# Gathering the tokens of a mixture of experts in four chunks of plain fp32, with nothing of the next stage emitted amid the experts

## The chip, the cores and the metric

One core of one Trainium2 chip runs the whole kernel. Its engines are TensorE (PE, with its weight loads PEld), VectorE (DVE), ScalarE (ACT), GpSimd (POOL) and SyncE (SP), which issues most DMAs. The metric is the device time of one execution in microseconds (us), the median of several runs.

## What is computed

256 tokens of width 1024 pass through ten stages. Stages 0 to 5 are two transformer blocks of a first kind (SwiGLU, token mixer, SwiGLU, twice). Stages 6 to 9 are a second kind: attention, mixture of experts (MoE), attention, MoE. Each stage is modulated by a vector that is a product of a conditioning vector with a 1024x6144 matrix (`ada_w`). All weights are fp32 in HBM. The MoE, of which the change speaks:

```
h = rms_norm_2(x, norm_ffn_g[i]) * (1.0 + sc2) + sh2
x = x + g2 * grouped_moe(h, router_w, router_bias, moe_w_gate[i], moe_w_up[i], moe_w_down[i])

def grouped_moe(h, ...):
    scores = sigmoid(t @ router_w)          # 16 experts; one group, top 2 inside it
    ...
    for e in range(N_EXPERTS):
        he = silu(t @ w_gate[e]) * (t @ w_up[e])
        out = out + gates[:, e:e + 1] * (he @ w_down[e])
```

Each expert has 1024x512, 1024x512 and 512x1024 weights, so a MoE stage reads 192 pieces of 512 KB.

## The kernel before

**Order.** Nothing is left to a scheduler: each engine runs its instructions in the order in which the Python code emits them, and an engine waits at an instruction until its operands and its target buffer are ready.

**Weights as a stream.** Weights come as "units" of 128x1024 fp32 (512 KB) in the order of use, through one pool of equal buffers (`s4`, `S4_BUFS` of them, 4 KB in each partition). SP issues the loads (line 76, tile `raw`). Three kinds of unit follow each other:

- Normal units are split in two: ACT makes `hi` (line 117) and DVE `lo` (line 122); PE then takes three products of one pass each (lines 325 to 327).
- Units of `ada_w` are worked off by DVE alone (line 414, or 412 for the first of a vector: multiply and add into `aacc`). When a vector is complete, PE sums it over the partitions (line 421).
- Units of the experts are plain: PE multiplies by them as they are.

`stream.ahead(n)` splits up to n units that have been loaded and loads further ones as long as the pool has more free buffers than `self.reserve`; of units that are not plain, only a few wait loaded and unsplit. `pump()` calls it after each step with a credit that grows by `self.rate`. A second pool (`t2`, 2 KB in each partition, `T2_BUFS`) holds small tiles.

**The MoE stages (7 and 9).** `route` normalises x to `xn`, computes the scores and lays the tokens into 16 x 64 slots: a slot table that says which of 256 tokens sits in which slot. Two experts make a pair (128 slots), two pairs a chunk of 256 slots. A chunk is gathered by multiplying the tokens by a one-hot matrix `OH`; the product goes through ACT or DVE (modulation) into `hg`. Before the change xn is split into two parts of one-pass precision, `xs` (`high` on ACT, line 1833; `low` on DVE, line 1837), and each of the eight k steps of a chunk takes four one-pass matmuls of 256 columns (line 1660). Chunk 0 is gathered ahead of the pairs, chunks 1 to 3 amid them. The DMA of xn to HBM (`xd`, line 1943, on ACT's queue, four of them) and of the row of the gate `g2` (`row`, line 449) stand around there as well.

`pairs` then emits eight pairs. For pair j: `G(j)`, the gate product of 32 matmul instructions (line 1575); `X(j-1)`, transposes of the pair before; G again for the up product; `Dn(j-1)`, the down product (line 1594, 32 instructions); and what adds pair j-1 into x: `Y` (lines 1602 to 1608) and `S` (PE line 1615, then DVE `x <- x + psacc`, line 1617). Gathering steps and S steps wait in a queue, of which `tick` takes one after every quarter (8 instructions) of a G or a Dn. After pair 7 come X(7), Dn(7) and a tail: the S of pair 6, and Y and S of pair 7, after which x is complete. Then the next stage normalises x, transposes it (line 376) and starts with its products.

Of the kernel before, what the change touches and what calls it, by code (L numbers as in the profile page):

```python
# [11 lines left out]
F32 = mybir.dt.float32  # L12
# [9 lines left out]
P = 128  # L22
D = 1024
# [9 lines left out]
S4_BUFS = 39  # L33
T2_BUFS = 14
# [148 lines left out]
class Net:  # L183
# [261 lines left out]
    def row(self, st):  # L445

        self.need(st, "row")
        r = self.s4([P, D], F32, "row")
        self.nc.sync.dma_start(r, self.rowd.pop((st, "row")).rearrange("a b -> (a b)").partition_broadcast(P))
        return r  # L450
# [757 lines left out]
    def proj_halves(self, st, hT):  # L1208
# [32 lines left out]
        self.rate, self.reserve = 0, 17  # L1241
# [318 lines left out]
    def pairs(self, hg, gsl, row, OHT, done):  # L1560
# [90 lines left out]

    def gather(self, c, OH, xs, hg, G, S):

        nc = self.nc
        s = slice(c * 256, (c + 1) * 256)
        for k in range(KC):
            ps = self.ps()
            for t in range(NT):
                for i in range(2):
                    nc.tensor.matmul(ps[:, :256], xs[i][t][:, k * P:(k + 1) * P], OH[t][:, s], start=t == 0 and i == 0, stop=t == 1 and i == 1)  # L1660
# [7 lines left out]
            yield  # L1668

    def slots(self, c, OH, gates, gsl, OHT):  # L1670

        nc = self.nc
        pg = self.ps()
        for i in range(2):
            j = 2 * c + i
            for t in range(NT):
                nc.tensor.matmul(pg[:, 2 * i:2 * i + 2], OH[t].bitcast(F32)[:, j * P:(j + 1) * P], gates[:, t, 2 * j:2 * j + 2], start=t == 0, stop=t == 1)
# [111 lines left out]
    def moe(self, st, pre, rest):  # L1789
# [10 lines left out]
        xn, xT, r, ss, junk, xs = {}, {}, {}, {}, {}, {}  # L1800
# [68 lines left out]
        high(0, 0)  # L1869
# [4 lines left out]
        low(0, 0)  # L1874
        high(0, 1)
# [38 lines left out]
        low(1, 0)  # L1914
# [41 lines left out]
        OHT = [self.s4([P, 4, 256], F32R, "OHT") for _ in range(2)]  # L1956
        self.reserve = 1
        gsl = self.sm(8, name="gsl", bufs=1)
        box = {}
        for c in range(4):  # L1960
            if c:
                self.side.append(lambda c=c: [hot(t, c) for t in range(NT)])
# [167 lines left out]
```

## Time and profile before

| what | us |
|---|---|
| median of 3 runs | 2264.72 (2261.26 to 2264.96) |
| profiled execution | 2252.76 |
| its span, first to last instruction | 2251.1 |
| PE busy | 2146.7 (95%) |
| DVE busy / ACT busy | 1367.0 (61%) / 906.2 (40%) |
| mean granted TensorE clock | 0.978 |
| stage 7: first gather matmul, first G, x complete | 1590.0, 1596.3, 1848.4 |
| stage 8: first transposes | 1852.75 |
| stage 9: first gather matmul, first G, x complete | 2007.0, 2013.0, 2244.3 |

The profiled execution has 1.7 us outside its span and lies 12 us below the median. A share of busy time is an average over the stages; in a MoE stage the DMA engines carry some 410 GB/s, in the others 90 to 320.

### The profile page before, as it was taken

How to read it: one execution, taken by the hardware profiler on the slowest of the kernel's cores; microseconds unless marked ns; L12 is line 12 of the kernel's file. 1: busy time of each engine (PE TensorE's matmuls, PEld its weight loads, DVE VectorE, ACT ScalarE, POOL GpSimd, SP SyncE). 2: the span in 40 equal slices, each digit the busy share in tenths (PEclk: the TensorE clock that was granted, in tenths of full speed). 3: DMA queues.
4: the chain of work that ended last, by engine and by line, in shares of the span. 5: the costliest groups of instructions: out<-in, count | busy, mean ns of one | idle time of the engine just before them, and what ended most of it. 6: DMA issues, size and time to landing. Idle time of an engine off the chain costs nothing. (4 is left out here: it accounts for less than half of the span.)

```text
span 2251.1 us, 28030 instructions
## 1 busy us (share of the span) xinstructions
PE 2146.7 (95%) x10326; PEld 1545.9 (69%) x10326; DVE 1367.0 (61%) x2125; ACT 906.2 (40%) x1603; POOL 92.6 (4%) x118
## 2 busy tenths in 40 slices
PE   8999999999999999999999999999899959989997
PEld 7888778787888788778878788776433327763332
DVE  6976767568865885776548875876322156542222
ACT  3543444555533544454455543553211025521110
POOL 0000000100000000000000000110000002000000
PEclk9999999999999999999999999998899979989999
DMA  9886667526886786576536787654799975659996
GB/s 374 317 297 227 253 208 251 174 96 253 321 279 214 270 309 222 195 269 214 194 103 243 282 290 241 203 195 187 290 409 409 409 276 191 228 183 409 409 409 273
DMA packets 166960, 595.15 MB, mean 264 GB/s; under 512 B 18744, under 2 KB 18832, under 8 KB 166816
## 3 DMA queue, kind: packets, MB, share of 16 engines
q1 hardware_dynamic: 163152, 583.21, 71.1%
q0 software_dynamic: 2064, 6.88, 1.1%
q10 hardware_dynamic: 1600, 3.19, 0.4%
q8 instruction: 84, 1.38, 0.2%
q14 instruction: 60, 0.49, 0.1%
HBM read 590.00 MB, written 3.20 MB: 264 GB/s over the span
## 5 line engine op out<-in xcount | busy, mean ns | idle before, releaser
L122 DVE TENSOR_TENSOR lo<-raw,hi 128x1024 fp32r<-128x1024 f32 x478 | 570.6, 1215 | 25.6 <-ACT hi L117 24.8
L325 PE MATMUL psw<-hi,hT 128*128 128x512 f32 (+1 forms) x1296 | 524.8, 405 | 9.2 <-ACT hT L580 8.2
L117 ACT CAST hi<-raw 128x1024 fp32r<-128x1024 f32 x478 | 478.4, 1046 | 90.2 <-DMA raw<-in_w_qkv_dram 31.4
L327 PE MATMUL psw<-lo,hT 128*128 128x512 f32 (+1 forms) x1296 | 507.1, 391 | 4.6 <-DVE lo L122 4.6
L326 PE MATMUL psw<-hi,hT 128*128 128x512 f32 (+1 forms) x1296 | 506.6, 391 | 0.0
L325 PEld LDWEIGHTS psw<-hi,hT 128*128 128x128 f32 x1296 | 244.6, 189 | 64.2 <-ACT hT L580 12.0
L327 PEld LDWEIGHTS psw<-lo,hT 128*128 128x128 f32 x1296 | 243.9, 188 | 58.1 <-DVE lo L122 6.3
L414 DVE SCALAR_TENSOR_TENSOR aacc<-raw,csil,aacc 128x1024 f32<-128x1024 f32 (+1 forms) x210 | 261.5, 1245 | 29.3 <-DMA raw<-in_ada_dram 28.8
L326 PEld LDWEIGHTS psw<-hi,hT 128*128 128x128 f32 x1296 | 244.8, 189 | 46.3
L1575 PE MATMUL psw<-raw,hg 128*64 128x512 f32 x1024 | 239.4, 600 | 0.0
L1575 PEld LDWEIGHTS psw<-raw,hg 128*64 128x64 f32 x1024 | 66.7, 136 | 119.1 <-issue 107.5
L1594 PE MATMUL psacc<-raw,gT 128*64 128x512 f32 x512 | 124.8, 609 | 22.0 <-DVE x L1617 20.0
L325 PE MATMUL psacc<-hi,gT 128*128 128x512 f32 x352 | 140.0, 398 | 4.2 <-ACT gT L688 4.2
L327 PE MATMUL psacc<-lo,gT 128*128 128x512 f32 x352 | 138.7, 394 | 1.3 <-DVE lo L122 1.3
L326 PE MATMUL psacc<-hi,gT 128*128 128x512 f32 x352 | 139.0, 395 | 0.0
L1617 DVE TENSOR_TENSOR x<-x,psacc 128x512 f32<-128x512 f32 x64 | 43.5, 686 | 141.9 <-PE psacc L1615 141.9
L651 ACT ACTIVATE sg<-psw 128x256 f32<-128x256 f32 x86 | 32.7, 383 | 185.9 <-PE psw L327 184.9
L652 DVE TENSOR_TENSOR sg<-psw,sg 128x256 f32<-128x256 f32 x86 | 36.1, 423 | 101.3 <-ACT sg L651 101.0
L520 POOL TENSOR_TENSOR r<-m,nhalf 128x1 f32<-128x1 f32 (+3 forms) x30 | 45.3, 1510 | 1198.4 <-DVE m L517 1180.7
L1594 PEld LDWEIGHTS psacc<-raw,gT 128*64 128x64 f32 x512 | 35.4, 138 | 84.9 <-issue 49.1
L1663 ACT ACTIVATE hg<-psw,mc,mc 128x256 f32<-128x256 f32 x32 | 18.0, 564 | 176.9 <-PE psw L1660 176.9
L688 ACT CAST gT<-psw 128x256 fp32r<-128x256 f32 x88 | 29.6, 374 | 136.7 <-PE psw L376 136.6
(330 smaller groups left out, 2620.1 us busy)
## 6 DMA issues: line engine op xcount, KB each, us to landing
raw<-in_ada_dram SPq DMA_DIRECT2D x224, 512.0 KB, 4.8
raw<-in_w_gu_dram SPq DMA_DIRECT2D x176, 512.0 KB, 5.3
raw<-in_moe_g_dram SPq DMA_DIRECT2D x128, 512.0 KB, 10.2
raw<-in_moe_u_dram SPq DMA_DIRECT2D x128, 512.0 KB, 10.2
raw<-in_moe_d_dram SPq DMA_DIRECT2D x128, 512.0 KB, 10.2
raw<-in_w_mix_dram SPq DMA_DIRECT2D x96, 512.0 KB, 5.0
raw<-in_w_dn_dram SPq DMA_DIRECT2D x88, 512.0 KB, 4.5
raw<-in_w_qkv_dram SPq DMA_DIRECT2D x48, 512.0 KB, 5.4
```

The source lines that it names most:

```text
L117: nc.scalar.copy(hi[:, :cols], raw[:, :cols])
L122: nc.vector.tensor_tensor(out=lo[:, :cols], in0=raw[:, :cols], in1=hi.bitcast(F32)[:, :cols], op=ALU.subtract)
L325: mm(ps, a[0], w[0], start=first, stop=False)
L326: mm(ps, a[1], w[0], start=False, stop=False)
L327: mm(ps, a[0], w[1], start=False, stop=last)
L414: nc.vector.scalar_tensor_tensor(out=acc, in0=raw, scalar=c, in1=acc, op0=ALU.mult, op1=ALU.add)
L520: nc.gpsimd.tensor_tensor(out=r, in0=m, in1=self.nhalf[:, :w], op=ALU.pow)
L651: nc.scalar.activation(sg[:, :256], ps[:, :256], AF.Silu)
L652: nc.vector.tensor_tensor(out=sg[:, 256:], in0=ps[:, 256:], in1=sg[:, :256], op=ALU.mult)
L1575: mm(ps[s], hg(k, j)[:, s], w[0][:, i * 512:(i + 1) * 512], start=k == 0, stop=k == KC - 1)
L1594: mm(yb[h][s], gT[:, f * P + s.start:f * P + s.stop], w[0][:, h * 512:(h + 1) * 512], start=f == 0, stop=f == 3)
L1617: nc.vector.tensor_tensor(out=self.x[:, t, s], in0=self.x[:, t, s], in1=ps, op=ALU.add)
```

## The change

Six things are changed. (1) The gather uses xn as it is, in plain fp32: two matmuls for a k step instead of four of one pass; xn, the one-hot matrix and its transpose now live in t2 tiles, and the tiles `xs` and the two `OH` in the large pool go. (2) `gather` and `slots` become `chunk`, which allocates `hg` for its own chunk, and takes two k steps at a time; chunk c is queued at pair 2c-2 (`ahead`). (3) The reserve of free buffers is 5 instead of 17 in the tail of the attention stage, no longer 13 in `route`, and 3, 2, 0, 7 later instead of 3, 1, 0, 7. (4) `self.rate` is 0 during the pairs. (5) The row's DMA goes to ACT's queue. (6) The pools have 38 and 16 buffers instead of 39 and 14.

```diff
-S4_BUFS = 39
-T2_BUFS = 14
+S4_BUFS = 38
+T2_BUFS = 16
...
-        self.rate, self.reserve = 0, 17
+        self.rate, self.reserve = 0, 5
...
         for j in range(8):
             self.until(("hg", j // 2))
-            if j == 6:
-                self.reserve = 7
+            ahead(j)
             pg = G(j)
...
-    def gather(self, c, OH, xs, hg, G, S):
+    def chunk(self, c, OH, xn, hg, G, S, gates, gsl, OHT):
+        oh = self.t2(name="OH")
+        for t in range(NT):
+            OH(oh, t, c)
+        yield
+        hg[c] = [self.s4([P, 4, 256], F32, "hg") for _ in range(2)]
         for k in range(KC):
             ps = self.ps()
             for t in range(NT):
-                for i in range(2):
-                    nc.tensor.matmul(ps[:, :256], xs[i][t][:, k * P:(k + 1) * P], OH[t][:, s], start=t == 0 and i == 0, stop=t == 1 and i == 1)
+                nc.tensor.matmul(ps[:, :256], xn[t, k // 4][:, (k % 4) * P:(k % 4 + 1) * P], oh[:, t * 256:(t + 1) * 256], start=t == 0, stop=t == 1)
...
-            yield
+            if k % 2:
+                yield
...
-        def high(t, q):
-            nc.scalar.copy(xs[0, t][:, q * 512:(q + 1) * 512], xn[t, q])
-
-        def low(t, q):
-            s = slice(q * 512, (q + 1) * 512)
-            nc.vector.tensor_tensor(out=xs[1, t][:, s], in0=xn[t, q], in1=xs[0, t][:, s].bitcast(F32), op=ALU.subtract)
...
-        self.reserve = 13
...
+        hg, OHT = {}, {}
+        chunks = [self.chunk(c, hot, xn, hg, G, S, lambda: v3(gz, 2), gsl, OHT) for c in range(4)]
+        while ("hg", 0) not in self.marks:
+            next(chunks[0])
         self.reserve = 3
...
-            if c == 0:
-                self.side.append(lambda: box.update(row=self.row(st)))
+        box = {"row": self.row(st, nc.scalar)}
+        self.reserve = 2
+        self.steps(chunks[0], 3)
+
+        def ahead(j):
+            if j % 2 == 0 and j < 6:
+                self.steps(chunks[j // 2 + 1], 7)
+            if j == 5:
+                self.reserve = 0
+            if j == 6:
+                self.reserve = 7
...
+        self.rate = 0
```

Three places show what moves. First DVE at the end of stage 7's pairs, before the change. `psacc` are the sums of S, `aacc` and `lo` belong to stage 8, `yg` and `yh` to the Y of pair 7:

```order
L1608 TENSOR_TENSOR yh3451_14898<-yg3449_14895,yh3450_14897 128x512
L1617 TENSOR_TENSOR x_77<-x_77,psacc3456_14918 128x512
L414 SCALAR_TENSOR_TENSOR aacc2851_12645<-raw3460_14934,csil_82,aacc2851_12645 128x1024
L1617 TENSOR_TENSOR x_77<-x_77,psacc3463_14941 128x512
L1617 TENSOR_TENSOR x_77<-x_77,psacc3466_14952 128x512
L122 TENSOR_TENSOR lo3465_14950<-raw3461_14937,hi3464_14949 128x1024
L1617 TENSOR_TENSOR x_77<-x_77,psacc3470_14966 128x512
L122 TENSOR_TENSOR lo3468_14961<-raw3462_14939,hi3467_14960 128x1024
L1639 SCALAR_TENSOR_TENSOR sg3474_14980<-psw3459_14929,gsl3142_13779,sg3474_14980 128x512
L414 SCALAR_TENSOR_TENSOR aacc2851_12645<-raw3473_14978,csil_82,aacc2851_12645 128x1024
```

The same place of the changed kernel, from the S of pair 5 on:

```order
L1617 TENSOR_TENSOR x_77<-x_77,psacc3457_14848 128x512
L1617 TENSOR_TENSOR x_77<-x_77,psacc3463_14868 128x512
L1617 TENSOR_TENSOR x_77<-x_77,psacc3465_14878 128x512
L1617 TENSOR_TENSOR x_77<-x_77,psacc3466_14886 128x512
L1638 SCALAR_TENSOR_TENSOR sg3467_14894<-psw3460_14859,gsl3120_13701,sg3467_14894 128x512
L1602 TENSOR_TENSOR yg3474_14928<-psacc3468_14897,row3137_13757 128x512
L1602 TENSOR_TENSOR yg3477_14937<-psacc3469_14898,row3137_13757 128x512
```

The first L414 of stage 8 stood between two S of pair 5 and is gone from there; the changed kernel has it, and every L122 of stage 8, behind the last L1617 of the stage. Of stage 8's units, eight splits and three ada steps stood ahead of that point before (and a ninth split right behind it), and none does now; four units (one of ada, three of `w_qkv`) are loaded by then.

Second, PE where chunk 1 is gathered amid a G of stage 7; before:

```order
L1660 MATMUL psw3158_13839<-OH3118_13699,xs3075_13576 128x256
L1575 MATMUL psw3155_13830<-raw3039_13412,hg3121_13707 64x512
L1575 MATMUL psw3155_13830<-raw3040_13414,hg3121_13707 64x512
L1575 MATMUL psw3155_13830<-raw3039_13412,hg3121_13707 64x512
L1575 MATMUL psw3155_13830<-raw3040_13414,hg3121_13707 64x512
L1660 MATMUL psw3161_13853<-OH3117_13698,xs3072_13573 128x256
L1660 MATMUL psw3161_13853<-OH3117_13698,xs3073_13574 128x256
L1660 MATMUL psw3161_13853<-OH3118_13699,xs3074_13575 128x256
L1660 MATMUL psw3161_13853<-OH3118_13699,xs3075_13576 128x256
L1575 MATMUL psw3155_13830<-raw3041_13416,hg3122_13708 64x512
```

And now:

```order
L1663 MATMUL psw3161_13830<-OH3153_13812,xn3086_13605 128x256
L1663 MATMUL psw3161_13830<-OH3153_13812,xn3095_13641 128x256
L1663 MATMUL psw3162_13834<-OH3153_13812,xn3086_13605 128x256
L1663 MATMUL psw3162_13834<-OH3153_13812,xn3095_13641 128x256
L1575 MATMUL psw3156_13819<-raw3039_13412,hg3124_13709 64x512
L1575 MATMUL psw3156_13819<-raw3040_13414,hg3124_13709 64x512
L1575 MATMUL psw3156_13819<-raw3039_13412,hg3124_13709 64x512
L1575 MATMUL psw3156_13819<-raw3040_13414,hg3124_13709 64x512
L1663 MATMUL psw3163_13842<-OH3153_13812,xn3086_13605 128x256
```

Four one-pass matmuls for one k step became four plain fp32 matmuls for two k steps; PE executes a plain fp32 matmul as two instructions, so a quarter of a G (8 instructions) stands here as four rows. A G is now interrupted four times for a chunk instead of eight.

Third, SP around the start of stage 7. `row` at line 449 is the gate row of stage 6 first, then that of stage 7; before:

```order
L76 DMA raw3058_13514<-in_moe_g_dram 128x1024
L449 DMA row3059_13516<-rowd2038_9042 128x1024
L76 DMA raw3147_13800<-in_moe_g_dram 128x1024
L76 DMA raw3149_13812<-in_moe_g_dram 128x1024
L76 DMA raw3150_13814<-in_moe_u_dram 128x1024
L449 DMA row3151_13816<-rowd2507_11128 128x1024
L76 DMA raw3152_13822<-in_moe_u_dram 128x1024
L76 DMA raw3156_13835<-in_moe_u_dram 128x1024
```

And now:

```order
L449 DMA row3058_13514<-rowd2037_9040 128x1024
L76 DMA raw3070_13565<-in_moe_g_dram 128x1024
L76 DMA raw3071_13567<-in_moe_g_dram 128x1024
L76 DMA raw3072_13572<-in_moe_g_dram 128x1024
L76 DMA raw3073_13574<-in_moe_u_dram 128x1024
L76 DMA raw3075_13579<-in_moe_u_dram 128x1024
L76 DMA raw3076_13581<-in_moe_u_dram 128x1024
L76 DMA raw3077_13583<-in_moe_u_dram 128x1024
L76 DMA raw3078_13585<-in_moe_u_dram 128x1024
L76 DMA raw3141_13768<-in_moe_u_dram 128x1024
L76 DMA raw3142_13770<-in_moe_u_dram 128x1024
L76 DMA raw3143_13772<-in_moe_u_dram 128x1024
```

The second row is no longer among SP's DMAs. The DMAs of all queues take turns on eight semaphores, so that SP's ninth DMA waits for whatever used its semaphore last. The four DMAs of xd, which ACT issues after chunk 0, hold such semaphores: before the change SP comes to the first of them with `raw3156`, its 27th expert unit or so, and now six units later.

## Rows read from the trace of the kernel before

**Rows 1.** Windows: us, busy us of PE, PEld, DVE, ACT, POOL, clock, DMA share, GB/s

```profile
1605.00:1785.00 180.00, 180.00 (x831) 67.17 (x828) 44.95 (x77) 23.75 (x41) 0.00 (x0) 1.00 1.03 409
1800.00:1820.00 20.00, 0.43 (x2) 0.29 (x4) 2.36 (x3) 1.04 (x1) 0.00 (x0) 0.57 1.03 410
```

**Rows 2.** Timeline at stage 7's end: start, us, engine, line, what; idle before

```profile
1786.96 19.54 SPq L76 DMA_DIRECT2D raw<-in_moe_d_dram  x16
...
1797.99 1.55 PE L1594 MATMUL psacc<-raw,gT 128*64 128x512 f32 x4
...
1817.64 1.28 DVE L414 SCALAR_TENSOR_TENSOR aacc<-raw,csil,aacc 128x1024 f32<-128x1024 f32 x1 [28.64 <-DMA raw<-in_ada_dram]
...
1819.57 8.09 PE L1594 MATMUL psacc<-raw,gT 128*64 128x512 f32 x28 [20.04 <-DVE x L1617]
...
1835.94 1.19 PE L1615 MATMUL psacc<-yh,OHT 128*128 128x512 f32 x4
...
1847.73 0.69 DVE L1617 TENSOR_TENSOR x<-x,psacc 128x512 f32<-128x512 f32 x1 [0.70 <-PE psacc L1615]
```

**Rows 3.** Timeline of chunk 0's gather in stage 9

```profile
2004.41 0.68 DVE L1837 TENSOR_TENSOR xs<-xn,xs 128x512 fp32r<-128x512 f32 x1
...
2006.97 6.07 PE L1660 MATMUL psw<-OH,xs 128*128 128x256 f32 x32 [2.15 <-DVE OH L1930]
...
2008.56 0.54 DVE L1665 TENSOR_SCALAR hg<-psw,mc,mc 128x256 f32<-128x256 f32 x1 [0.35 <-PE psw L1660]
...
2011.12 0.56 ACT L1663 ACTIVATE hg<-psw,mc,mc 128x256 f32<-128x256 f32 x1 [1.14 <-PE psw L1660]
...
2012.12 0.56 ACT L1663 ACTIVATE hg<-psw,mc,mc 128x256 f32<-128x256 f32 x1 [0.44 <-PE psw L1660]
...
2013.08 0.56 ACT L1663 ACTIVATE hg<-psw,mc,mc 128x256 f32<-128x256 f32 x1 [0.39 <-PE psw L1660]
```

**Rows 4.** Timeline of PE in a mixer stage

```profile
419.99 0.59 PE L935 MATMUL psacc<-sp,ntri 128*128 128x256 f32 x2
420.42 0.39 PE L938 MATMUL psacc<-sp,nones 128*128 128x128 f32 x2
```

**Rows 5.** Timeline of PE in stage 7, pairs 0 and 1

```profile
1601.56 5.37 PE L1575 MATMUL psw<-raw,hg 128*64 128x512 f32 x24
1606.86 0.74 PE L1660 MATMUL psw<-OH,xs 128*128 128x256 f32 x4
...
1609.39 0.74 PE L1660 MATMUL psw<-OH,xs 128*128 128x256 f32 x4
```

**Rows 6.** Timeline of SP's queue before stage 7's pairs

```profile
1578.27 21.96 SPq L76 DMA_DIRECT2D raw<-in_moe_u_dram  x4
```

**Rows 7.** Timeline at stage 9's end

```profile
2213.76 4.92 PE L1594 MATMUL psacc<-raw,gT 128*64 128x512 f32 x18
...
2223.31 0.66 PE L376 MATMUL psw<-ident,sg 128*128 128x128 f32 x4
2224.64 6.82 PE L1594 MATMUL psacc<-raw,gT 128*64 128x512 f32 x26 [0.68 <-ACT gT L1585]
...
2233.50 1.20 PE L1615 MATMUL psacc<-yh,OHT 128*128 128x512 f32 x4
...
2243.62 0.69 DVE L1617 TENSOR_TENSOR x<-x,psacc 128x512 f32<-128x512 f32 x1 [0.76 <-PE psacc L1615]
```

**Rows 8.** Timeline at stage 8's start

```profile
1852.75 1.94 PE L376 MATMUL psw<-ident,xn 128*128 128x128 f32 x8 [5.06 <-DVEq L2012]
...
1858.12 1.05 ACT L117 CAST hi<-raw 128x1024 fp32r<-128x1024 f32 x1
...
1867.00 1.03 PE L376 MATMUL psw<-ident,xn 128*128 128x128 f32 x8
```

**Rows 9.** Page, costliest groups: busy us, mean ns, idle before

```profile
L122 DVE TENSOR_TENSOR lo<-raw,hi 128x1024 fp32r<-128x1024 f32 x478 | 570.6, 1215 | 25.6 <-ACT hi L117 24.8
...
L327 PE MATMUL psw<-lo,hT 128*128 128x512 f32 (+1 forms) x1296 | 507.1, 391 | 4.6 <-DVE lo L122 4.6
```

More of the change, by code (lines that the diff above doesn't have):

```diff
@@ L443, in ada_items, with row @@
         return [(src[kc][:, i * w:(i + 1) * w], w, job(i, kc)) for i in range(parts) for kc in range(KC)]
-    def row(self, st):
+    def row(self, st, queue=None):
         self.need(st, "row")
         r = self.s4([P, D], F32, "row")
-        self.nc.sync.dma_start(r, self.rowd.pop((st, "row")).rearrange("a b -> (a b)").partition_broadcast(P))
+        (queue or self.nc.sync).dma_start(r, self.rowd.pop((st, "row")).rearrange("a b -> (a b)").partition_broadcast(P))
         return r
@@ L1558, in first_hit, with pairs @@
         return mx, r
-    def pairs(self, hg, gsl, row, OHT, done):
+    def pairs(self, hg, gsl, row, OHT, ahead, done):
         nc, mm = self.nc, self.nc.tensor.matmul
@@ L1676, in slots @@
             for t in range(NT):
-                nc.tensor.matmul(pg[:, 2 * i:2 * i + 2], OH[t].bitcast(F32)[:, j * P:(j + 1) * P], gates[:, t, 2 * j:2 * j + 2], start=t == 0, stop=t == 1)
+                nc.tensor.matmul(pg[:, 2 * i:2 * i + 2], oh[:, t * 256 + i * P:t * 256 + (i + 1) * P], gates()[:, t, 2 * j:2 * j + 2], start=t == 0, stop=t == 1)
         for h in range(2):
@@ L1685, in slots @@
             for t in range(NT):
-                j = 2 * c + i
-                nc.tensor.transpose(pt[:, (2 * i + t) * P:(2 * i + t + 1) * P], OH[t].bitcast(F32)[:, j * P:(j + 1) * P], self.ident)
-        nc.scalar.copy(OHT[c // 2][:, 2 * (c % 2):2 * (c % 2) + 2], pt.rearrange("p (j q) -> p j q", j=2))
+                nc.tensor.transpose(pt[:, (2 * i + t) * P:(2 * i + t + 1) * P], oh[:, t * 256 + i * P:t * 256 + (i + 1) * P], self.ident)
+        OHT[c] = self.t2(F32R, name="OHT")
+        nc.scalar.copy(OHT[c], pt)
         yield
@@ L1868, in moe @@
         logits(0, 1)
-        high(0, 0)
         square(1, 1)
@@ L1955, in moe @@
         nc.vector.tensor_tensor(out=v3(gz, 2), in0=v3(gz, 2), in1=ws[:, :, None].broadcast_to([P, 2, 16]), op=ALU.mult)
[L1956 to L1962, printed above, removed]
-                self.steps(self.gather(c, OH, xx, hg, G, S), KC)
-            self.steps(self.slots(c, OH, v3(gz, 2), gsl, OHT), 2)
-            if c == 0:
-                self.side.append(lambda: box.update(row=self.row(st)))
-        self.side.append(lambda: (self.free(*xs.values(), *OH), setattr(self, "reserve", 0)))
+        box = {"row": self.row(st, nc.scalar)}
[8 more added lines that the diff above has]
+                self.reserve = 7
         bmax = self.sm(1, name="bmax")
@@ L1976, in slots_of @@
             return hg[j // 2][k // 4][:, k % 4, (j % 2) * P:(j % 2 + 1) * P]
-        self.pairs(slots_of, gsl, lambda: box["row"], lambda j: OHT[j // 4][:, j % 4], lambda j: j % 2 and self.free(*hg[j // 2]))
+        self.rate = 0
+        self.pairs(slots_of, gsl, lambda: box["row"], lambda j: OHT[j // 2][:, (j % 2) * 256:(j % 2 + 1) * 256], ahead, lambda j: j % 2 and self.free(*hg[j // 2]))
         self.flush()
@@ L2015, in moe @@
         self.rate = 1
-        self.free(box["row"], *OHT)
+        self.free(box["row"])
         return nxt, lambda n: lambda: nxt and self.normed(nxt, 1, rs[1])
```

26 lines of the change are left out of this document (4 added, 22 removed).

## The prediction

> **What bounds the kernel now.** I read the windows by stage first, since a share of the whole span mixes stages with different limits. In the pairs of stage 7 PE is busy 180.00 of 180 us while the DMA engines run at 409 GB/s [rows 1]: two limits at once, a unit of 512 KB every 1.28 us and PE without a gap. Then come 20 us in which PE works 0.43 us and DVE 2.36 us, and the DMA goes on at 410 GB/s [rows 1]. The timeline says why [rows 2]: Dn(6) starts at 1797.99 with its first four instructions; the other 28 follow at 1819.57, after 20.04 us of waiting for an L1617 of DVE; and DVE had sat 28.64 us at its L414, which waits for a unit of `ada_w`. That unit stands on SP's queue behind 16 units of `moe_d` that took from 1786.96 on to issue. So DVE, which executes in order, holds the additions into x behind a step of the next stage, these hold PSUM buffers, and PE stands. The DMA is not idle: it brings the weights that PE needs next. A stall of 20 us is therefore worth less than 20, down to what those loads allow.
>
> **The change, part by part.**
>
> *The stall.* With `rate` 0 no L414 and no L122 stands amid the pairs. A Dn or G that isn't interrupted takes 32 instructions; 24 take 5.30 us [rows 5], so 32 take 7.07. From X to the next Dn there are 1.33 us (2223.31 to 2224.64) [rows 7]. Dn(6), X(7) and Dn(7) need 7.07 + 1.33 + 7.07 = 15.5 us, so Dn(7) could end at 1797.99 + 15.5 = 1813.5 instead of 1835.94. But the 16 units of `moe_d` are issued until 1806.5 and land some 10 us later: by DMA alone the end would be about 1817.5, some 18 us earlier than now. That is the bound of this gain. What replaces the stall: the L414 now stands behind the last L1617 and its unit, issued right behind `moe_d`, has landed long before.
>
> *Chunk 0 in plain fp32.* The gather runs from 2006.97 and its eviction steps come at 0.85 us each up to 2011.12 (2008.56 to 2011.12 is three steps), at 0.48 after (2012.12 to 2013.08 is two) [rows 3]: PE had been waiting, and I read this as the granted clock's lower level (1.2 GHz) for some 4.2 us, then its upper (2.4). A plain fp32 matmul of 256 columns is two instructions, and two of these take 0.43 us in a mixer stage (419.99 to 420.42) [rows 4]. A k step has two such matmuls: 0.86 us instead of 0.48, and 1.72 at the lower clock. In 4.2 us some 2.5 steps get done, the other 5.5 take 4.7: 8.9 us instead of 6.1, so +2.8. Ahead of it the L1837 go out of DVE's chain of routing; two of 0.68 us [rows 3] stand within that chain, one of them mostly beside PE's counting, so I take back 0.6. First G: +2.2 us, in both MoE stages.
>
> *Chunks 1 to 3.* Amid a G a k step and 8 instructions take 2.53 us (1606.86 to 1609.39), 8 instructions alone 1.77 [rows 5]: the step costs 0.76, of which 0.48 are its own and 0.28 the interruption. Now two steps come at once: 2 x 0.86 + 0.28 = 2.00 us, four times a chunk: 8.0 us instead of 8 x 0.76 = 6.1. For three chunks +5.7 us, in both stages, and PE has no gap there to hide it [rows 1].
>
> The price of fp32 is where a rule speaks against the change. The row gives 0.86 for 0.48, a factor of 1.8. The Trainium skill, "FP8 and Floating Point Precision", section TensorE Precision Notes, says that true fp32 takes four passes through the array; two such matmuls are eight passes for the four of before, a factor of 2, so an estimate by that page is twice the old step, and the case is priced from rows among the rivals. The sum goes by the row.
>
> *What the loads gain.* SP issues expert units ahead until it comes to a semaphore that xd holds, and then stands for about 20 us [rows 6]. By the order it now gets six units further: 6 x 1.28 = 7.7 us of lead, less the 2.2 by which xd comes later: 5.5. So stage 7's last weights land near 1812. PE reaches Dn(6) at 1797.99 + 2.2 + 5.7 = 1805.9 and ends Dn(7) at 1821.4: now PE is the later one, by some 9 us, and the lead is cover, not gain. Without any lead the loads would end at 1819.7, which changes nothing either.
>
> *Stage 7 in sum.* Dn(7) ends at 1821.4 instead of 1835.94, -14.5. The tail from there to the last addition into x takes 12.5 us in stage 7 (1835.94 to 1848.42) [rows 2] and 10.8 in stage 9 (2233.50 to 2244.31) [rows 7]; stage 7's has the L421 sum of stage 8's vector and splits among it, which move out: -1.7. Together -16.2.
>
> *Stage 9.* There is no next stage, so no stall to lose. Dn(6) starts at 2213.76 and Dn(7) ends at 2233.50 [rows 7], 19.7 us where 15.5 would do: 4.2 us of waiting for `moe_d`. With PE 7.9 us later and the loads 5.5 earlier these go: 7.9 - 4.2 = +3.7.
>
> *Stage 8's start.* Before, nine units were split when PE came to stage 8 at 1852.75, and its first two products of token tile 0 (16 steps over eight units) ran without a wait until 1867.00 [rows 8]. Now four units lie loaded and none is split, since the splits stand behind the transposes' work on ACT and DVE. ACT gets to its first `hi` where it had one before, at 5.4 us after the transposes' start (1858.12), and needs 1.05 us [rows 8]; then DVE makes eight `lo` of 1.22 us [rows 9], with two ada steps of at most 1.28 [rows 2] between them: 1859.17 + 9.8 + 2.6 = 1871.5, and half a microsecond of products behind the last one: 1872.1 instead of 1867.0, **+5.1**. Lower bound: the first split cannot be there before 1859.17 + 1.22 = 1860.4, where the products before began behind the transposes (1852.75 + 1.94 = 1854.7) and were well on by then, so at least 3. Upper bound: everything that was done ahead lies bare, nine splits and three ada steps, 9 x 1.22 + 3 x 1.28 = 14.8. I take 5.1, since DVE was nearly idle while PE went through these products before. The L421 sum moved here costs its 1.7 again. Together +6.8.
>
> *The rest.* One buffer fewer in the large pool shifts loads by an instruction or two in all stages; PE waits only 4.6 us in all for `lo` there [rows 9], and I take +0.5 (0 to 3). The row's DMA on ACT's queue stands behind xd and is wanted only at the first Y, a G and more later: nothing. The t2 pool has two more buffers and holds four xn, an OH and two OHT more during the pairs; tiles wait for a free one only if DVE or ACT are late, and they are busy a quarter of these windows [rows 1]: nothing, at most 2.
>
> **Sum:** -16.2 + 3.7 + 6.8 + 0.5 = -5.2 us. Against the profiled execution of 2252.8 that is 2247.6. The median of the runs shown is 12 us above it, and the same difference gives about 2259.5 there.
>
> **Rivals.**
>
> *Stage 8's start costs little.* If ACT and DVE catch up within the first product (DVE had hardly anything to do there), the lag is 2 or less and the L421 hides: about -10, 2255. For it: the four loaded units need no wait. Against it: `hi` and `lo` for two units are made no faster than PE uses them.
>
> *Stage 8's start costs all that was done ahead.* PE stands between splits, so its clock falls as it does ahead of a gather [rows 3], and the second token tile meets DVE still behind: 14.8 instead of 5.1, sum +4.5, 2269. For it: both tiles use the same units, and DVE has its transposes' work in between.
>
> *Fp32 costs twice the old step.* The row that gives 0.43 us ends at a matmul of another kind, which may start early. At 2 x 0.48 = 0.96 us a step, chunk 0 takes 0.9 more (2.2 steps in 4.2 us, 5.8 x 0.96 after) and the other 24 steps 2.4: +3.3 in each stage, sum +1.4, 2266. It is what the page named above would make of it.
>
> *One buffer fewer, the slower side.* Stages 0 to 6 run splits and loads through the same pool for 1590 us. If PE's waits for `lo` grow from 4.6 us by more than 10, that decides: slower by 0.2%. Nothing in the rows says that the pool is short there; one load later by an instruction, 400 units long, would have to cost 25 ns each.
>
> *The wait only changes its cause.* Something else keeps DVE's additions or Dn waiting and the stall remains: -5.2 + 14.5 and more, 2274. The order shows no instruction of the next stage left between the additions, so I give it little.
>
> **How the numbers follow.** A measurement of this kernel tells about 0.2%, 4.5 us, from no change. The sum as worked out gets 0.51, with a range of its own from -10 to 0 (a lag of 3 to 8, the buffer at 0 to 3); six tenths of that lie beyond -4.5. The little lag gets 0.20, the full lag 0.13 (half of it within the bound), the dearer fp32 0.07, the buffer 0.06, the unchanged wait 0.03. Faster: 0.31 + 0.20 = 0.51; same: 0.20 + 0.07 + 0.07 = 0.34; slower: 0.06 + 0.06 + 0.03 = 0.15. The likeliest is 2259.5; to leave no more than 2 in 10 out I go from 2251 to 2270.
>
> **What would show it.** In the profile after: PE without a wait for L1617 near stage 7's end and x complete near 1832; L1663 steps of about 2.0 us for two k steps amid G; first G 2.2 us later after the gather's start; PE waiting for `hi` and `lo` at stage 8's start, and the second transposes there 19 to 20 us after the first instead of 14.3; Dn(7) of stage 9 without waits for `moe_d`. The prediction is wrong if the fp32 steps cost well off 0.86 us, if stage 8 recovers or multiplies its lag, or if stages 0 to 6 move by more than a few us.

## Result and profile after

The changed kernel takes 2278.62 us (median of 7 runs, 2276.32 to 2288.32); the kernel before, run beside it, takes 2260.42 (7 runs, 2252.28 to 2264.96). The ratio is 1.0099, 95% interval 1.0074 to 1.0124: slower by 1%, where 2259.5 and a range of 2251 to 2270 had been forecast. The profiled execution of the changed kernel takes 2278.01 us (span 2276.3), 25 us more than the profiled one of before.

The windows by stage come first: stages 0 to 5, stage 6, stage 7 (from its gather to stage 8's first transposes), stage 8's start, the rest of stage 8, stage 9. The columns are the window, its length, busy time of PE, PEld, DVE, ACT, POOL with their instructions, granted clock, DMA share, GB/s. Before:

```profile
0.00:1457.00 1457.00, 1415.13 (x6901) 1162.85 (x6902) 1034.42 (x1500) 699.04 (x1182) 53.10 (x92) 1.00 0.69 242
1457.00:1590.00 133.00, 119.45 (x570) 88.01 (x569) 92.90 (x184) 60.00 (x134) 18.81 (x12) 0.89 0.54 193
1590.00:1852.80 262.80, 234.83 (x1057) 91.86 (x1058) 80.63 (x141) 42.11 (x69) 1.10 (x2) 0.94 0.93 370
1852.80:1867.00 14.20, 14.20 (x57) 11.57 (x57) 6.15 (x21) 4.42 (x11) 1.65 (x1) 0.83 0.44 149
1867.00:2007.00 140.00, 130.61 (x706) 102.42 (x704) 88.04 (x164) 70.70 (x156) 17.93 (x11) 0.97 0.58 203
2007.00:2244.30 237.30, 232.50 (x1040) 89.22 (x1040) 64.84 (x119) 29.93 (x52) 0.00 (x0) 0.98 0.94 372
```

The same view of the changed kernel:

```profile
0.00:1469.40 1469.40, 1421.31 (x6901) 1168.05 (x6902) 1035.02 (x1500) 700.48 (x1182) 52.32 (x92) 0.99 0.69 240
1469.40:1602.60 133.20, 121.06 (x571) 88.92 (x569) 91.23 (x181) 57.91 (x130) 19.40 (x12) 0.89 0.60 217
1602.60:1847.20 244.60, 237.07 (x1041) 95.54 (x1041) 66.86 (x126) 32.96 (x60) 1.30 (x2) 0.98 0.93 365
1847.20:1867.40 20.20, 15.65 (x57) 12.15 (x58) 17.12 (x31) 11.98 (x19) 1.00 (x1) 0.71 0.85 316
1867.40:2027.10 159.70, 147.58 (x722) 113.28 (x720) 89.30 (x165) 69.59 (x153) 17.29 (x12) 0.87 0.59 201
2027.10:2269.60 242.50, 238.36 (x1040) 95.92 (x1040) 64.09 (x118) 30.07 (x52) 0.00 (x0) 0.98 0.90 354
```

The lengths differ by +12.4, +0.2, -18.2, +6.0, +19.7 and +5.2 us, in sum +25.3. Forecast were about +0.5, 0, -16.2, +5.1, +1.7 and +3.7. The MoE stages and stage 8's start went as forecast to within 2 us; the loss sits in the two windows that the prediction had priced at next to nothing.

Stage 7's end in the changed kernel, PE's timeline (start, length, instruction, in brackets idle time before it and its releaser), answers to [rows 2]:

```profile
1817.95 7.04 PE L1594 MATMUL psacc<-raw,gT 128*64 128x512 f32 x32
1824.92 0.66 PE L376 MATMUL psw<-ident,sg 128*128 128x128 f32 x4
1826.25 7.09 PE L1594 MATMUL psacc<-raw,gT 128*64 128x512 f32 x32 [0.67 <-ACT gT L1585]
1833.27 1.19 PE L1615 MATMUL psacc<-yh,OHT 128*128 128x512 f32 x4
```

The 20-us wait for L1617 is gone, no wait for `moe_d` is left, and Dn(6), X(7), Dn(7) take 15.3 us (forecast 15.5). From the first G to Dn(7)'s end are 221.7 us, 239.7 before.

The gathers (stage 7's chunk 0, the first G, two pieces of chunk 1 amid a G; then stage 9's chunk 0), answering to [rows 3, 5]:

```profile
1602.59 9.06 PE L1663 MATMUL psw<-OH,xn 128*128 128x256 f32 x32 [2.01 <-DVE OH L1912]
...
1622.19 1.99 PE L1663 MATMUL psw<-OH,xn 128*128 128x256 f32 x8
1624.11 1.94 PE L1575 MATMUL psw<-raw,hg 128*64 128x512 f32 x8
1625.98 2.00 PE L1663 MATMUL psw<-OH,xn 128*128 128x256 f32 x8
...
2027.10 10.13 PE L1663 MATMUL psw<-OH,xn 128*128 128x256 f32 x32 [2.01 <-DVE OH L1912]
```

Chunk 0 takes 9.0 us in stage 7, where it took 6.2, and 10.1 in stage 9, where it took 6.0. Two k steps with eight instructions of G take 3.79 us (1622.19 to 1625.98); with 1.77 for the eight alone, two steps cost 2.02, and 2.00 was forecast. So a step takes 0.87 us of its own; the factor of 2 that the Trainium skill's page "FP8 and Floating Point Precision", TensorE Precision Notes, gives by its four passes would be 2.20 for the two. The trace stands by the row.

Stage 8's start, answering to [rows 8]:

```profile
1847.19 1.94 PE L376 MATMUL psw<-ident,xn 128*128 128x128 f32 x8 [4.11 <-DVEq L1992]
1853.64 0.80 PE L325 MATMUL psw<-hi,hT 128*128 128x512 f32 x1 [4.51 <-ACT hi L117]
```

PE waits 4.51 us for the first `hi`, once, and then catches no further wait, none for a `lo` either; the second transposes follow at 1867.39, 20.2 us after the first (14.2 before). The wait makes 4.5 of these 6.0 us. The other 1.5 are PE's busy time (15.65 for 14.20), with more of it at the lower clock (0.71 for 0.83 granted).

### The profile page after: what moved, and what is told of

It reads as the page before. It is cut to its first block, busy times and chain, and to the rows that moved or that the text cites. A ratio compares the mean times of both kernels' runs of the same rounds, so it can differ in the third digit from the quotient of the medians.

```text
span 2276.3 us, 27990 instructions
## 1 busy us (share of the span) xinstructions
PE 2181.0 (96%) x10326; PEld 1573.9 (69%) x10326; DVE 1363.7 (60%) x2117; ACT 903.0 (40%) x1595; POOL 91.3 (4%) x118
## 5 line engine op out<-in xcount | busy, mean ns | idle before, releaser
L122 DVE TENSOR_TENSOR lo<-raw,hi 128x1024 fp32r<-128x1024 f32 x478 | 570.7, 1216 | 32.3 <-ACT hi L117 32.3
L327 PE MATMUL psw<-lo,hT 128*128 128x512 f32 (+1 forms) x1296 | 509.9, 393 | 10.8 <-DVE lo L122 10.7
L327 PEld LDWEIGHTS psw<-lo,hT 128*128 128x128 f32 x1296 | 245.3, 189 | 66.8 <-DVE lo L122 15.3
L414 DVE SCALAR_TENSOR_TENSOR aacc<-raw,csil,aacc 128x1024 f32<-128x1024 f32 (+1 forms) x210 | 261.8, 1247 | 0.7 <-DMA raw<-in_ada_dram 0.2
L1617 DVE TENSOR_TENSOR x<-x,psacc 128x512 f32<-128x512 f32 x64 | 43.6, 688 | 151.9 <-PE psacc L1615 151.9
L1594 PE MATMUL psacc<-raw,gT 128*64 128x512 f32 x512 | 116.4, 597 | 1.3 <-ACT gT L1585 1.3
L325 PEld LDWEIGHTS psacc<-hi,gT 128*128 128x128 f32 x352 | 66.8, 190 | 22.2 <-ACT gT L688 4.9
## 6 DMA issues: line engine op xcount, KB each, us to landing
raw<-in_moe_g_dram SPq DMA_DIRECT2D x128, 512.0 KB, 10.2
raw<-in_moe_u_dram SPq DMA_DIRECT2D x128, 512.0 KB, 10.2
raw<-in_moe_d_dram SPq DMA_DIRECT2D x128, 512.0 KB, 10.2
```

What stands on the lines that cost most here:

```text
L122: nc.vector.tensor_tensor(out=lo[:, :cols], in0=raw[:, :cols], in1=hi.bitcast(F32)[:, :cols], op=ALU.subtract)
L325: mm(ps, a[0], w[0], start=first, stop=False)
L327: mm(ps, a[0], w[1], start=False, stop=last)
L414: nc.vector.scalar_tensor_tensor(out=acc, in0=raw, scalar=c, in1=acc, op0=ALU.mult, op1=ALU.add)
L1594: mm(yb[h][s], gT[:, f * P + s.start:f * P + s.stop], w[0][:, h * 512:(h + 1) * 512], start=f == 0, stop=f == 3)
L1617: nc.vector.tensor_tensor(out=self.x[:, t, s], in0=self.x[:, t, s], in1=ps, op=ALU.add)
```

## Where the loss builds up

**Stages 0 to 5: +12.4 us.** PE's busy time is up by 6.2 us (1415.13 to 1421.31) at equal instructions, its idle time by 6.2. The idle time is in the waits; first before, then after, each for its window of stages 0 to 5 (us in total, times, longest):

```profile
PE psw L327 <- DVE lo L122: 4.6, 3, 1.6
```

```profile
PE psw L327 <- DVE lo L122: 10.7, 6, 3.0
```

The first new place is in stage 1, the first mixer. It is the 102nd split of the run; DVE's `lo` of it, before:

```profile
357.31 1.22 DVE L122 TENSOR_TENSOR lo<-raw,hi 128x1024 fp32r<-128x1024 f32 x1
```

And in the changed kernel, with PE's product that needs it:

```profile
371.69 1.22 DVE L122 TENSOR_TENSOR lo<-raw,hi 128x1024 fp32r<-128x1024 f32 x1
372.96 0.50 PE L327 MATMUL psw<-lo,hT 128*128 128x512 f32 x1 [2.07 <-DVE lo L122]
```

The stage runs only 0.6 us late up to there, but the split comes 14 us later, behind other work of DVE: `ahead` splits and loads only while enough buffers are free. Whether the buffer is the cause is for the experiments to say.

**Stage 8 after its start: +19.7 us.** Of these 17.0 are PE's busy time (130.61 to 147.58). The records of PE differ by 16 (722 for 706), the 16 matmuls of the L421 sum that moved in from stage 7, worth 1.8 us; the other 15 belong to the same matmuls as before. The windows of the changed kernel around 1954 us show how:

```profile
1900.00:1915.00 15.00, 11.76 (x51) 8.96 (x50) 8.41 (x9) 7.43 (x15) 2.53 (x3) 0.89 0.54 134
1947.00:1954.50 7.50, 7.50 (x53) 6.63 (x52) 4.50 (x6) 4.68 (x7) 0.00 (x0) 1.00 0.97 373
1954.60:1985.30 30.70, 30.70 (x96) 19.87 (x94) 11.69 (x19) 9.05 (x33) 0.00 (x0) 0.50 0.44 163
```

The corresponding work before:

```profile
1945.00:1975.00 30.00, 30.00 (x182) 22.64 (x183) 14.81 (x30) 13.78 (x44) 0.00 (x0) 1.00 0.74 277
```

For 30.7 us PE is busy without a gap at a granted clock of 0.50, its lower level (1.2 GHz), and gets 96 records done where 182 were done before, in 30 us from the same place on. What ran ahead of it, from PE's timeline of the changed kernel:

```profile
1951.80 1.00 PE L856 MATMUL psacc<-v,pT 128*128 128x64 f32 x8
1952.64 1.90 PE L421 MATMUL psw<-ones,aacc 128*128 128x1 f32 x16
1954.40 0.89 PE L376 MATMUL psw<-ident,yt 128*128 128x128 f32 x4
1955.08 1.81 PE L856 MATMUL psacc<-v,pT 128*128 128x64 f32 x8
1956.68 0.42 PE L456 MATMUL psw<-ident,mc 128*8 128x128 f32 x1
1956.90 3.51 PE L856 MATMUL psacc<-v,pT 128*128 128x64 f32 x16
1960.34 0.79 PE L816 MATMUL psacc<-qk,qk 64*128 64x128 f32 x2
```

The sum of a vector (16 matmuls of one column) stands here between attention's products of 64 columns. Before, it stood behind products of 512 columns, but what followed it was much the same:

```profile
1944.37 1.84 PE L421 MATMUL psw<-ones,aacc 128*128 128x1 f32 x16
1946.07 1.98 PE L856 MATMUL psacc<-v,pT 128*128 128x64 f32 x16
1947.89 0.27 PE L456 MATMUL psw<-ident,mc 128*8 128x128 f32 x1
1947.99 1.90 PE L856 MATMUL psacc<-v,pT 128*128 128x64 f32 x16
...
1952.40 0.47 PE L325 MATMUL psacc<-hi,yT 128*128 128x512 f32 x1
```

Here PE ran for 8 us without a product of 512 columns, and the clock stayed at 1.00; in the changed kernel it fell within 3 us of the last such product. So narrow products alone did not bring the lower level. Nor is such a stretch new. Before the change, stage 6, the other attention stage, has one of 20.5 us in the same profile:

```profile
1530.00:1550.00 20.00, 20.00 (x51) 10.58 (x51) 11.30 (x20) 7.71 (x27) 0.00 (x0) 0.50 0.24 86
```

The window 1900 to 1915 holds a smaller loss, some 5 us: ACT waits 6.53 us for an L824 of DVE, and PE 3.24 us for a `hi` behind it.

## Experiments

Each run stands beside the kernel before on the same chip; ratios are to that.

### One buffer fewer, nothing else (e1_one_buffer_fewer)

```diff
-        self.live4 = 0
+        self.live4 = 1
...
+            if st == 6:
+                self.live4 -= 1
```

> The kernel before, whose plan for the large pool counts one buffer as taken until stage 6 begins (39 stay allocated, 38 are used); nothing else. Theory A (the buffer): loads and splits of stages 0 to 6 come later in the engines' order, PE waits for lo and hi near 370, 409, 545, 1147 and 1240 us as in the changed kernel, stage 7's gather starts some 12 us later, and the whole takes about 12 us more than before. Rival B (the 12 us of stages 0 to 6 are no matter of the plan but of the execution's clock, or of the second pool): no change beyond 4 us.

2265.19 us; ratio 1.0058, interval 1.0041 to 1.0076. PE's waits for `lo` in stages 0 to 5 rise to 11.9 us, and the lag against the trace of before appears at the same places as in the changed kernel (370, 409, 545, 1240 us). In stages 0 to 5 the large pool has no spare buffer: one fewer there costs 0.6%. The split shown above comes at 371.57 us in this trace and holds PE for the same 2.07 us.

### Rate 0 amid the pairs, nothing else (e2_rate_zero_alone)

```diff
+        self.rate = 0
```

> The kernel before with the credit for splits at 0 during the pairs; the gather, the reserves and the pools as before. Theory A (the four prices add up): the wait of 20 us for L1617 goes, Dn(7) of stage 7 ends 16 to 18 us earlier, x is complete some 18 us earlier, stage 8's first products take 6 us longer, so about 11 us less in all if nothing else moves. Rival B (splits that come late at stage 8's start set off the long stretch at half clock near its middle): stage 8 shows 30 us at a granted clock of 0.5 with PE busy, which costs 15, and the whole takes about 4 us more than before.

2251.68 us; ratio 0.9997 (0.9974 to 1.0019). The end of stage 7 in its timeline:

```profile
1805.81 2.84 PE L1594 MATMUL psacc<-raw,gT 128*64 128x512 f32 x10
1808.86 2.35 PE L1594 MATMUL psacc<-raw,gT 128*64 128x512 f32 x8 [0.21 <-DMA raw<-in_moe_d_dram]
...
1826.08 1.20 PE L1615 MATMUL psacc<-yh,OHT 128*128 128x512 f32 x4
```

The stall is gone, Dn(6) to Dn(7)'s end takes 20.3 us with waits for `moe_d` between: the bound by the loads that the prediction gave (1817.5 - 1797.99 = 19.5). Stage 7 is 19.7 us shorter in the profile (243.0 for 262.7), stage 8's start 6.3 longer, and the rest of stage 8 2.1. In the median hardly anything of the 11 us left is to be seen. In this profile the lower clock held for 44.3 us in stages 0 to 5, against 10.2 in that of before (table below). The ten runs of this one kernel spread with the clock, from 2240.61 us at a mean of 0.981 to 2261.89 at 0.969.

### The change with the pools of before (e3_changed_39_14)

```diff
-S4_BUFS = 38
-T2_BUFS = 16
+S4_BUFS = 39
+T2_BUFS = 14
```

> The changed kernel with the pools of before, 39 and 14 buffers. Theory A (the buffer costs 12 us in stages 0 to 6): stage 7's gather starts at about 1590 again and the whole takes some 12 us less than the changed kernel, about 10 us over before; the second pool's 14 buffers cost nothing. Rival B: the loss of stages 0 to 6 stays. Rival C (the gather needs the 16 small buffers): waits of PE for yh or OHT appear amid the pairs, 5 us or more.

2252.57 us; ratio 0.9989 (0.9974 to 1.0004). With 39 and 14 buffers the change costs nothing measurable; the waits for `lo` in stages 0 to 5 are back at 4.6 us. The changed kernel stands at 1.0099, so the sizes of the two pools, and they alone, make the whole loss. Which of the two does it behind stage 5 isn't separated: e1 takes a buffer from the large pool only, and gives it back at stage 6. Stage 8 still has a stretch of 20.5 us at the lower clock.

### The changed kernel again, and more work for the tail

> The changed kernel once more, on the chip of the next three. Theory A (long stretches at half clock with PE busy, in the attention stages, belong to this order of instructions): its profile shows two of 20 to 31 us again, near 1541 and 1955 us, mean clock 0.965 to 0.972, and it takes 1% more than before. Rival B (they fall by chance of the execution): the profile has one or none, and the time lies 10 to 15 us lower.

2280.83 us; 1.0116 (1.0099 to 1.0133). Its stretch in stage 8 starts at 1959.0 and again lasts 30.7 us, so it isn't a chance of one execution. The mean clock of each run bears this out: 0.965 to 0.971 in the eleven runs of the changed kernel, 0.973 to 0.980 in the ten of e3. At 2276 us, 0.970 for 0.977 is some 30 us more at the lower level, an estimate from these means, and the profiles of the two differ by as much (stage 6: 23.9 and 6.8 us; stage 8 after its start: 34.1 and 20.5). So the pool sizes cost clock as well as waits.

```diff
             for t in range(NT):
                 S(7, t, h)
+                self.stream.ahead(1)
```

> The kernel before with the credit at 0 during the pairs, and one split asked for after each of the four last S of pair 7. Theory A (the lag at stage 8's start is the lack of splits): three units are ready when stage 8 starts, its first two products take 15 to 17 us instead of 20.5 from the first transposes to the second, x of stage 7 is complete as early as with the credit alone, and the whole is 4 us below the credit alone. Rival B (splits amid the tail hold the last additions): x is complete 3 us later and nothing is gained.

> The changed kernel with pools of 39 and 14, and the same splits after the last four S. Theory A: 4 us below the changed kernel with pools of 39 and 14, that is some 6 us below before. Rival B: no change against it, since ACT's hi wait for their loads there.

The first (before, rate 0, one split after each S of the tail) takes 2251.49 us, ratio 0.9982 (0.9966 to 0.9999), the second (the change with 39 and 14 buffers and these splits) 2260.36, 1.0014 (0.9992 to 1.0037). Stage 8's start shrinks to 15.0 us in both, but its first transposes come 5.5 us after x is complete where 3.4 were, and the stretches at the lower clock in stage 8 are 10.2 and 27.3 us. What the splits win there is lost again. Of the 4 us that each was expected to gain, the first shows 3 by the ratios, within the intervals, and the second none.

### The fp32 gather alone (e7_fp32_gather_alone)

```diff
-                for i in range(2):
-                    nc.tensor.matmul(ps[:, :256], xs[i][t][:, k * P:(k + 1) * P], OH[t][:, s], start=t == 0 and i == 0, stop=t == 1 and i == 1)
+                nc.tensor.matmul(ps[:, :256], self.xng[t, k // 4][:, (k % 4) * P:(k % 4 + 1) * P], OH[t].bitcast(F32)[:, s], start=t == 0, stop=t == 1)
...
+        self.xng = xn
```

> The kernel before, whose gather multiplies plain xn and one-hot in fp32 (two matmuls a k step, one k step at a time as before); the split xs is still made. Theory A: a k step takes 0.86 instead of 0.48, first G 2.8 us after the old place in both stages, 24 x 0.38 = 9 us more in each stage's pairs; in stage 7 all of it hides behind the stall, which ends when the ada unit lands, so x of stage 7 is complete at most 3 us later; in stage 9 the waits for moe_d take up 4, and the whole takes about 8 to 10 us more. Rival B (fp32 costs twice, 0.96): 4 us more than that.

2268.28 us; 1.0051 (1.0034 to 1.0068), 12 us in the medians where 8 to 10 were expected. The k steps are still taken one at a time here, so each of the 24 amid the pairs costs 0.38 us more, where the changed kernel's cost 0.24 more. Stage 9 grows by 7.8 us (237.3 to 245.1): chunk 0 takes 3.1 more, the way from the first G to Dn(6) 9.5 more (24 x 0.38 = 9.1), and 4.4 are saved since the waits for `moe_d` behind it are gone here too. Stage 7 grows by 2.2 only, as the stall takes up the rest: its wait for L1617 is 11.71 us instead of 20.04.

```profile
1822.71 1.03 PE L1594 MATMUL psacc<-raw,gT 128*64 128x512 f32 x4
1835.45 8.08 PE L1594 MATMUL psacc<-raw,gT 128*64 128x512 f32 x28 [11.71 <-DVE x L1617]
```

### One buffer fewer in stages 0 and 1 (e10_one_fewer_stage_1)

The edit of e1, ended with `if st == 2:`.

> The kernel before, whose plan counts one buffer as taken until stage 2 begins. Theory A (stage 1, a mixer, is where the pool is short): PE is 7 us late by 410 us, as with one fewer until stage 6, and the whole takes 6 to 8 us more. Rival B (the loss builds up in all stages): 3 us or less.

2263.49 us; 1.003 (1.0014 to 1.0046). In the medians that is 7 of e1's 11 us, by the ratios about half, so stages 0 and 1 alone bring half of e1's loss or more. The waits for `lo` stand at 10.3 us, near e1's 11.9.

### Moving the sums of the vectors (e8, e9, e11, e12)

```diff
-                self.soon(lambda: col(i), 4)
+                self.soon(lambda: col(i), 1 if key[0] >= 8 else 4)
```

e11 and e12 have 10 in place of 1; e9 joins the edit with those of e2 and e5. The edit moves the last six sums: two in stage 8, and also four between about 1390 and 1505 us, which the expectations don't say.

> The changed kernel, with the sums of the ada vectors of stages 8 and 9 (line 421, matmuls of one column) asked for one step after the last unit instead of four, so that they stand between products of 512 columns and no longer amid the small matmuls of the attention. Theory A (that passage without a wide product starts the 31 us at half clock in stage 8): the stretch near 1955 goes or falls to 10 us or less, stage 8 gets some 10 to 15 us shorter, the whole about 2268. Rival B (the stretch has another cause): it stays within 5 us of its length and the time within 4 us of 2280.

> The kernel before with the credit at 0 amid the pairs, splits after the last four S, and those sums earlier too. Theory A: no stretch at half clock in stage 8 with PE busy, stage 8 as short as before or 1 us less, x of stage 7 complete 15 us earlier net of the start; the whole 8 us or more below before. Rival B: as without the earlier sums, 4 us below before, with a spread of 15 us between executions.

> The changed kernel, but the sums of the vectors of stages 8 and 9 (16 matmuls of one column, L421) come ten steps after their last unit instead of four. In stage 8 they then stand between products of 512 columns, as in the kernel before, and no longer with L856 and L376 alone around them. Theory A (a piece of PE's order without large products around L421 starts stage 8's stretch at the lower clock): no such stretch of more than 10 us in stage 8, the stage after its start takes about 145 us instead of 159.7, the median is 12 to 15 us below the changed kernel's, some 0.3 to 0.6% above the kernel before (what one buffer fewer costs stays). Theory B (the stretch belongs to stage 8's lag or to chance, not to the order there): a stretch of 20 us or more stays, and the ratio to the kernel before stays near 1.010.

> The changed kernel with the pools of before (39 and 14) and with the same later sums. If both causes are named rightly and add up, the loss is gone and what stages 7 and 9 and stage 8's start gain together shows: as the runs with the pools of before stood 0.1 to 0.3% below the kernel before with a 20 us stretch in stage 8, and such a stretch costs about half its length, the ratio is about 0.995, 2243 to 2248 us, and stage 8 shows no stretch of more than 10 us. Rival: the later sums cost as much as the stretch, or the stretch comes anyway: 0.998 to 1.002.

| kernel | median us | ratio | interval |
|---|---|---|---|
| e8: changed, sums earlier | 2274.64 | 1.0067 | 1.0043 to 1.0091 |
| e9: before, rate 0, tail splits, sums earlier | 2242.42 | 0.9954 | 0.9928 to 0.998 |
| e11: changed, sums later | 2275.98 | 1.0095 | 1.0073 to 1.0116 |
| e12: changed, 39/14, sums later | 2266.35 | 1.006 | 1.0036 to 1.0084 |

With another place of the sum the stretch is another: in e8 it is 20.5 us (at 1962.7), in e9 6.8, in e11 the windows of stage 8 after its start show 10.2 us of it, which begin a microsecond after the end of the sum (1979.48 to 1981.32):

```profile
1878.30:1982.60 104.30, 99.25 (x494) 75.70 (x492) 63.59 (x96) 54.39 (x119) 16.15 (x10) 0.97 0.55 182
1982.60:1992.80 10.20, 10.20 (x30) 6.31 (x30) 3.95 (x6) 3.67 (x11) 0.00 (x0) 0.50 0.67 241
1992.80:2030.90 38.10, 30.43 (x200) 26.99 (x199) 21.77 (x64) 11.83 (x24) 1.11 (x2) 0.90 0.75 278
```

That part takes 152.6 us there instead of 159.7, where 145 was expected, and the median shows nothing of it. e12 missed its expectation by more than 1%: e3 without this edit was at 0.9989. In its profile stage 6 takes 137.4 us, 30.7 of them at the lower clock, in e3's 126.3 with 6.8. So with a later sum the stretch in stage 8 is shorter, but that is no remedy; and as the edit moves sums of stage 6 too, it isn't a test of stage 8 alone. e9 beats both kernels, before by 0.5% and the changed one by about 1.4%; it has neither the fp32 gather nor the smaller pool. Its lead goes with the clock: a median of 0.9805 over its ten runs, where before has 0.9735 beside it and e5, which differs from it only in the place of the sums, 0.974.

### All profiles side by side

Lower clock is the time at a granted clock of 0.5, summed from each trace's record of it (stages 6 and 8, the latter after its start: without the stretch around the idle time ahead of the next gather).

| kernel | stages 0 to 5, us | of it lower clock | stage 6, us | of it lower clock | stage 8 after its start, us | of it lower clock |
|---|---|---|---|---|---|---|
| before | 1457.0 | 10.2 | 133.0 | 20.5 | 140.0 | 0 |
| e7 | 1470.1 | 44.3 | 133.6 | 23.9 | 140.0 | 0 |
| e2 | 1469.8 | 44.3 | 127.5 | 6.8 | 142.1 | 0 |
| e5 | 1463.0 | 27.2 | 127.4 | 6.8 | 147.2 | 10.2 |
| e9 | 1454.2 | 6.8 | 130.9 | 10.2 | 146.7 | 6.8 |
| e3 | 1462.8 | 27.2 | 126.3 | 6.8 | 149.8 | 20.5 |
| e6 | 1454.1 | 6.8 | 131.9 | 20.5 | 153.4 | 27.3 |
| e12 | 1459.2 | 13.6 | 137.4 | 30.7 | 152.4 | 13.6 |
| e1 (38 buffers) | 1469.4 | 23.8 | 133.6 | 23.9 | 140.0 | 0 |
| e10 (38 in stages 0, 1) | 1470.2 | 37.4 | 134.9 | 27.3 | 140.0 | 0 |
| changed (38) | 1469.4 | 27.2 | 133.2 | 23.9 | 159.7 | 34.1 |
| e4 (38) | 1472.8 | 34.0 | 134.3 | 27.3 | 159.7 | 34.1 |
| e8 (38) | 1474.0 | 40.8 | 135.9 | 23.9 | 147.9 | 20.5 |
| e11 (38) | 1482.0 | 51.1 | 131.3 | 10.2 | 152.6 | 17.0 |

With 39 buffers, stages 0 to 5 lie near a line: from e9 (6.8, 1454.2) to e7 (44.3, 1470.1) a microsecond at the lower clock costs 0.42; e2, e3, e5 and e6 are within 0.3 us of it, before and e12 lie 1.4 and 2.1 above. The kernels with 38 lie above it by 6.5 (changed), 7.1, 5.4, 9.0 and 8.0 (e1). That is the buffer's price in these stages once the clock is taken out: 6 to 7 us beside the others, about as much as PE's idle time grew (6.2). e10 lies 3.0 above, too near to e12 to read a share of stages 0 and 1 from it.

The buffer costs clock besides. Right behind the wait of 2.07 us shown above, the lower level holds for 3.4 us in each of the six profiles with one buffer fewer, and the other eight have neither that wait nor the lower level near it.

How long the lower clock holds in these stages varies for one and the same program part (6.8 to 44.3 us with 39 buffers), and so it does in stage 6: before, e2, e5 and e7 have the same instructions there, and 20.5, 6.8, 6.8 and 23.9 us of it. That is how executions differ, and why a difference of two profiles needs these columns beside it.

## Why the prediction was wrong

- **The stall and the tail of stage 7, -16.2:** right; the window shrank by 18.2 us. The price by the loads was right too (e2), and so was that PE, not the loads, would end it here.
- **Fp32, 2.00 us for two steps amid G and +2.8 for chunk 0:** right, 2.02 and, in stage 7, +2.7. The rival of twice the step is out.
- **Stage 9, +3.7:** +5.2. The waits for `moe_d` at its end went, as forecast (Dn(6) to Dn(7)'s end 15.3 us for 19.7), and the pairs up to Dn(6) cost 5.6 for 5.7. Chunk 0 cost +4.1 there, where 2.8 less 0.6 had been counted.
- **Stage 8's start, +5.1:** +6.0, so both rivals on the lag are out. The size is right and in part luck: the sum let DVE's chain of eight `lo` and two ada steps hold PE, and PE waited for none of them. It waited 4.5 us for the first `hi`, which came 6.4 us after the transposes' start, earlier than the lower bound's 7.7 for the first `lo`, and lost 1.5 by its clock.
- **"The rest": one buffer fewer, +0.5 (0 to 3).** This step failed. The argument was that PE waits only 4.6 us in all for `lo` [rows 9], so the pool isn't short. A small sum of waits can belong to a pool that just suffices; it says nothing of what one buffer less does. The waits rose to 10.7 us, stages 0 to 5 lie 6 to 7 us higher at equal clock, and the buffer alone, taken up to stage 6, costs 11 us in the medians, 13 by the ratio (e1). That alone lifts the sum of -5.2 to the range's upper end or beyond it. Under the change the two pool sizes together cost 25 us, 1.0099 for 0.9989: with the pools of before the same change (e3) comes out inside the range. The rival had named the mechanism, though by waits it asked for more than 10 us and they grew by 6.1, and had got a chance of 0.06.
- **Stage 8 behind its start: not in the sum but for 1.7.** This failed as well, in the profile. The forecast followed the lag to the second transposes and let the stage end there, though rate 0 and the new reserve move what comes after: which units lie split, when the vector is complete, and so where its sum stands on PE. The stage took 19.7 us more, 15 of them the lower clock on PE; with the pools of before (e3) it is 9.8.

By the profile's windows, with stages 0 to 5 alone at equal clock: 6 - 18.2 + 6.0 + 19.7 + 5.2 = 18.7 us, beside 18 in the medians. In e3 the 6 go and stage 8 after its start takes 149.8: -18.1 + 6.0 + 9.8 + 5.0 = 2.7, where the medians show -2, about no change. Its stage 6 is left out of this sum; it was 6.7 us shorter than before, with 6.8 us at the lower clock for 20.5.

e1's median is 11 us above before, and 6 to 7 are seen as waits. Its four runs were granted 0.974 in the median, the nineteen of before beside it 0.976: an estimate from these means is 10 us more at the lower level, worth 4 at 0.42 each, which makes the rest.

What stays open is what starts the stretch in stage 8. The four profiles with the order of before have none, nine of the ten with rate 0 have 7 to 34 us, so it goes with that order; but e2 has none, moving the sum shortens it without ending it, and the trace of before has the sum followed by 8 us of narrow products at full clock. That the sum of one-column matmuls amid small products causes it is thus not shown, and the trace of before speaks against it as the whole cause. Why the smaller large pool, or the larger small one, makes it 30.7 us for e3's 20.5 wasn't tested.

## What to carry to other kernels

A buffer taken from a pool that feeds the critical engine is to be priced as a risk of its own, and tried alone: a small sum of waits doesn't show spare room. Follow a moved step to the end of the stage that it was moved into, since the order behind it shifts too. And before two profiles are compared, take the time at the lower clock out of both; here it varies by 37 us in stages 0 to 5 between executions, worth 16 us, nearly as much as the change. The mean clock of every run helps where only one of them was profiled.

## What the runs showed of the hardware

TensorE's clock fell to 0.50, its lower level, while PE, by the profile, was busy without a gap: it had been busy 7.50 of 7.50 us at 1.00 just before, and was so for 30.70 of 30.70 us in the stretch (again 30.7 in the second profile). It rose again only after tens of microseconds, though products of 512 columns ran within the stretch. What ran before the fall were products of 64 columns and one column, but the trace of before shows such a passage of 8 us at full clock. The Trainium skill's page "TensorE: Matmul & The Clock Gate", Part 1, ties the lower level to idling, and tells of waits for loads and of short idling between groups of matmuls as what brings it. This trace shows a fall without a wait of PE, so here the measurement decides: half the clock can be lost without one. It means some 15 us in stage 8, most of what the end of the stall gave back. The other kind shows too: behind PE's wait of 2.07 us in stage 1 the lower level held for 3.4 us in all six profiles that have the wait.
